# A row-wise nanmax on one core: the wait for the last store moved to GpSimd, into a critical section of its own

One Trainium2 chip, one core of it. The metric is the time of one execution on the device in microseconds (us), the median over several executions. The profile is of one execution; its span runs from the first to the last instruction of the program.

## The reference

```python
def setup_inputs():
    batch, seq, dim = 32, 2048, 2048
    x = np.random.randn(batch, seq, dim).astype(np.float32)
    mask = np.random.rand(batch, seq, dim) < 0.1
    x[mask] = np.nan
    return {"x": x, "axis": -1}

def reference(x, axis):
    return np.nanmax(x, axis=axis).astype(np.float32)
```

537 MB are read and 0.26 MB written, so the kernel is a stream of loads with just enough arithmetic beside it: on the page of the kernel before, the DMA engines are busy for 90% or more in 39 of 40 slices, and the three compute engines for 79 to 93% of the span.

## The kernel before

ScalarE and GpSimd turn NaNs into a very low number by arithmetic on the upper halves of the floats, and VectorE takes the maximum of each row. All loads and stores are issued by SyncE. The kernel does its own synchronization: everything stands in one critical section, in which a small class (`Order`) sets each wait and each semaphore increment. Only the end of the section matters here:

```python
    with tc.tile_critical():
        order = Order(nc)
        # ... loads, ScalarE, GpSimd and VectorE work, all waits explicit (cut) ...
        for (og, bits), e in zip(stores, ready):
            last = order.add(
                "sp",
                nc.sync,
                lambda: nc.sync.dma_start(out=og, in_=bits),
                [e],
                lane="store",
                step=16,
            )
        nc.sync.wait_ge(order.sems[last[0]], last[1])
```

There are five stores on one semaphore. Each adds 16, and the wait is for 80, so for all of them. The framework wraps the section. At its exit the section's *sync engine* (SyncE, unless told otherwise) raises a semaphore (a counter that others wait on), every engine that takes part answers with a drain, and the sync engine collects the answers. I call these the announcement, the drains and the collecting waits. After the last section the program ends with two all-engine barriers, run by GpSimd, with a semaphore clear between them.

## Time and profile before

| | before |
|---|---|
| median of 3 runs | 1253.81 us (1253.79 to 1254.08) |
| span of the profiled run | 1251.8 us |
| last vector instruction ends | 1248.81 us |
| last store: issue begins / has landed | 1248.84 / 1250.50 us |
| landing to end of span ("the tail") | 1.28 us |

The first two rows are the timed runs and the page; the others come from the trace's records of single instructions and of the store's semaphore, which have starts in nanoseconds. The store raises its semaphore in 16 updates; "landed" is the last of them. In the lines shown, DVE is VectorE, ACT ScalarE and POOL GpSimd; SPq, POOLq and PEldq are the sequencers (the instruction queues) of SyncE, GpSimd and TensorE. The prediction below shows the lines of the page and of the last microseconds.

### The profile page before, as it was taken

The page shows a single profiled execution, that of the slowest core. Times are in us where ns is not written, and L with a number is a line of the kernel's source. Part 1 is how long each engine was busy: PE and PEld are TensorE (multiplying, and loading weights), DVE is VectorE, ACT ScalarE, POOL GpSimd, SP SyncE. Part 2 cuts the span into 40 slices and gives each one's busy share as a digit, 9 for nine tenths or more (in the row PEclk, how much of TensorE's full clock was granted, in tenths as well). Part 3 has the DMA queues.
Part 4 walks back from the last instruction along what each step waited for, and adds up shares of the span by engine and source line. Part 5 has one row for each costly group of instructions (what it writes and reads, how often), then busy time and mean ns, then how long its engine had stood idle before and what let it go on. Part 6 is the DMA issues. An engine that isn't in the chain of part 4 may idle for free.

```text
span 1251.8 us, 872 instructions
## 1 busy us (share of the span) xinstructions
DVE 1110.5 (89%) x169; ACT 988.5 (79%) x271; POOL 1166.9 (93%) x239
## 2 busy tenths in 40 slices
DVE  0888989888889988898988888998888899999999
ACT  3777887778787877788777877787777878989997
POOL 2999989998999899998999899989999999999997
DMA  9999999999999999999999999999999999999997
GB/s 415 440 421 429 440 440 440 424 427 440 440 440 427 424 440 440 438 431 421 440 440 438 432 420 440 440 438 434 418 440 440 436 438 421 431 434 426 430 427 289
DMA packets 16279, 537.20 MB, mean 429 GB/s; under 512 B 2448, under 2 KB 2448, under 8 KB 3472
## 3 DMA queue, kind: packets, MB, share of 16 engines
q1 hardware_dynamic: 16272, 537.14, 99.3%
q14 instruction: 7, 0.06, 0.0%
HBM read 536.87 MB, written 0.26 MB: 429 GB/s over the span
## 4 chain that ended last, share of the span: by engine, by line
DVE 37%; DMA 35%; POOL 17%; ACT 10%; issue 1%; SPq 0%; DVEq 0%
DVE acc L194 37%; DMA xt<-in_x_dram 35%; POOL xt L190 17%; ACT kt L186 9%; ACT xt L186 1%; SPq L228 0%; DVE none L194 0%; DVEq L124 0%; SPq L384 0%; SPq L182 0%
## 5 line engine op out<-in xcount | busy, mean ns | idle before, releaser
L190 POOL TENSOR_SCALAR xt<-kt 128x3584 int16<-128x3584 uint16 (+8 forms) x235 | 1166.7, 4965 | 78.7 <-ACT kt L186 60.1
L194 DVE TENSOR_REDUCE acc<-xt 128x3 f32<-128x6144 f32 (+4 forms) x164 | 1108.8, 6807 | 137.1 <-POOL xt L190 127.7
L186 ACT ACTIVATE kt<-xt,scalars 128x3584 uint16<-128x3584 int16 (+9 forms) x248 | 936.0, 3812 | 255.8 <-DMA xt<-in_x_dram 237.9
L186 ACT ACTIVATE xt<-kt 128x3584 int16<-128x3584 uint16 (+4 forms) x21 | 53.5, 2545 | 0.7
L186 ACT ACT_TABLE_LOAD x1 | 1.3, 1283 | 0.9 <-SPq L182 0.9
L196 DVE MEMSET scalars<- 128x1 f32 x1 | 0.1, 59 | 1.0 <-SPq L182 1.0
L194 DVE TENSOR_SCALAR none<-acc 128x414 int32<-128x414 f32 (+1 forms) x2 | 0.9, 428 | 0.1
L194 DVE TENSOR_TENSOR acc<-acc,none 128x414 int32<-128x414 int32 (+1 forms) x2 | 0.8, 422 | 0.1
L370 POOL MEMSET const-float32-0.0<- 128x1 f32 x1 | 0.1, 99 | 0.2 <-issue 0.2
L186 ACT ACTIVATE scalars<-scalars 128x1 f32<-128x1 f32 x1 | 0.2, 202 | 0.0
L370 POOL MEMSET const-bfloat16-1.0<- 128x1 bf16 x1 | 0.1, 102 | 0.0
L370 POOL MEMSET const-uint8-127<- 128x1 uint8 x1 | 0.1, 102 | 0.0
L370 POOL MEMSET const-float32-1.0<- 128x1 f32 x1 | 0.1, 99 | 0.0
## 6 DMA issues: line engine op xcount, KB each, us to landing
xt<-in_x_dram SPq DMA_DIRECT2D x61, 7168.0 KB, 22.5
xt<-in_x_dram SPq DMA_DIRECT2D x12, 1024.0 KB, 27.5
xt<-in_x_dram SPq DMA_DIRECT2D x5, 2048.0 KB, 22.0
xt<-in_x_dram SPq DMA_DIRECT2D x2, 4864.0 KB, 18.9
xt<-in_x_dram SPq DMA_DIRECT2D x2, 3584.0 KB, 22.0
xt<-in_x_dram SPq DMA_DIRECT2D x3, 2304.0 KB, 20.4
xt<-in_x_dram SPq DMA_DIRECT2D x5, 1280.0 KB, 26.3
xt<-in_x_dram SPq DMA_DIRECT2D x1, 4608.0 KB, 18.5
```

The costliest lines, as they stand in the source:

```text
L186: return order.add("act", nc.scalar, lambda: nc.scalar.activation(**kw), deps)
L190: "pool", nc.gpsimd, lambda: nc.gpsimd.tensor_scalar(**kw), deps
L194: return order.add("dve", nc.vector, lambda: do(**kw), deps)
L196: e_top = order.add("dve", nc.vector, lambda: nc.vector.memset(top, EDGE), [])
L370: nc = _bacc.Bacc("TRN2", target_bir_lowering=False, num_devices=1)
```

## The change

The intent: SyncE leaves the first section without waiting for the store, so the section's exit runs while the store is in flight, and one engine alone then waits for the store in a second section.

```diff
                 lane="store",
                 step=16,
             )
-        nc.sync.wait_ge(order.sems[last[0]], last[1])
+
+    with tc.tile_critical(sync_engine=mybir.EngineType.Pool):
+        nc.gpsimd.wait_ge(order.sems[last[0]], last[1])
```

## The prediction

> **What bounds the kernel now.** I read the page first, from the span down to the chain that ended last, then the timeline of the last microseconds, then the sync engine's own waits, and last the instructions of the two lines that make the closing sequence.
>
> ```profile
> span 1251.8 us, 872 instructions
> DVE 1110.5 (89%) x169; ACT 988.5 (79%) x271; POOL 1166.9 (93%) x239
> DMA  9999999999999999999999999999999999999997
> HBM read 536.87 MB, written 0.26 MB: 429 GB/s over the span
> DVE 37%; DMA 35%; POOL 17%; ACT 10%; issue 1%; SPq 0%; DVEq 0%
> ```
>
> The reader is to see that the load stream sets the length. 536.87 MB at 429 GB/s is 1251 us, the whole span, and the row of DMA shares shows the queues over 90% busy in 39 of 40 slices. The three compute engines keep up with it at 79 to 93%. The change touches none of that: it moves one wait that stands after the last store is issued. So the stage to read is the last slice, and in it only what follows the final vector instruction. In the fourth row the sync engine's sequencer (SPq) has 0% of the chain, which already says how little is there.
>
> The timeline of the last microseconds shows where that stage begins:
>
> ```profile
> 1243.70 4.52 DVE L194 TENSOR_REDUCE acc<-xt 128x1 f32<-128x2048 f32 x2
> 1248.25 0.26 DVE L194 TENSOR_SCALAR none<-acc 128x98 int32<-128x98 f32 x1
> 1248.55 0.26 DVE L194 TENSOR_TENSOR acc<-acc,none 128x98 int32<-128x98 int32 x1
> 1248.84 0.33 SPq L348 DMA_DIRECT2D out_dram<-acc  x1
> ```
>
> GpSimd's last piece of work ends at 1245.8 us, ScalarE's at 1245.8, VectorE's at 1248.8. The last store is issued at 1248.84. From there to the end of the span is 1251.8 - 1248.84 = 2.96 us, and all of the change lies inside these 2.96 us, 0.24% of the span. The sync engine's waits split them:
>
> ```profile
> SPq L182 <- DMA out_dram<-acc: 1.3, 1, 1.3
> SPq L384 <- PEq L384: 0.5, 2, 0.4
> ```
>
> The first row is the wait that is moved. It lasts from the end of the issue (1248.84 + 0.33 = 1249.17) to the landing, 1.7 us after the issue began by the DMA issues (1248.84 + 1.66 = 1250.50). What is left, 1251.8 - 1250.5 = 1.3 us, is a closing sequence of semaphores. Its instructions, from the views of lines L182 (first section's exit) and L384 (end of the program) over that window:
>
> ```profile
> L182 SPq COMPARE_BRANCH  x1: 37/37/37, 1250.5 to 1250.5; - x1
> L182 SPq EVENT_SEMAPHORE  x3: 17/17/28, 1250.7 to 1250.9; - x3
> L182 POOLq DRAIN  x1: 41/41/41, 1250.7 to 1250.7; - x1
> L182 SPq NOP  x1: 18/18/18, 1251.0 to 1251.0; - x1
> L384 SPq DRAIN  x3: 7/7/7, 1251.1 to 1251.4; - x3
> L384 POOLq EVENT_SEMAPHORE  x4: 17/17/17, 1251.2 to 1251.7; - x4
> ```
>
> The branch at 1250.5 is the one that waits for the store. The records hold starts to the nanosecond, which narrow windows give to hundredths: branch 1250.51, SyncE's announcement 1250.68, one drain on each of four engines 1250.72 to 1250.77, SyncE's collecting waits 1250.85, 1250.91 and 1250.98, its drains 1251.06 and 1251.13, and GpSimd passing the first all-engine barrier at 1251.16. After that two barriers with a semaphore clear between them take 1251.8 - 1251.16 = 0.6 us; they stay as they are.
>
> [...] 49 KB, 1.7 us to landing. It is the same in both kernels, since the store is still issued by SyncE. [...] the rows have 7 to 41 ns each, yet the steps between them are 40 to 170 ns. I therefore cost steps from start to start, not durations. [...] SyncE's announcement at 1250.68 starts the others' drains at 1250.72, 40 ns. [...] the branch at 1250.51 is followed after 0.165 us, and the one on GpSimd at the start (0.76 to 0.96) after 0.20 us.
>
> **The change part by part.** The comparison of instruction order shows the same instructions on every engine up to the last store; by counts, the program has 8 more on GpSimd, 2 on SyncE and one on each of the others, all behind the last store.
>
> 1. Removed: SyncE's wait for the store before the first section's exit. That exit (announcement, four drains, three collecting waits, a NOP) now starts when the last store is issued, at 1249.17, and needs about what it needs now, 1251.06 - 1250.51 = 0.55 us; it ends near 1249.7, hidden beside the 1.3 us of flight. From the path this takes the 0.55 us from the landing to SyncE's first closing drain. Also GpSimd has been idle since 1245.8, so nothing delays its arrival.
>
> 2. Added before the wait: GpSimd's entry to the second section, a NOP and three waits at about 0.08 us each (two consecutive GpSimd semaphore instructions in the closing barrier start at 1251.16 and 1251.24). All but the last are done by 1250.0, also hidden.
>
> 3. Added after the landing, on the path. GpSimd sees the store at 1250.51 (20 ns after the landing, as SyncE does). Then 0.08 us to its branch, 0.165 to 0.20 us to the instruction after it, its announcement, at 1250.76 to 1250.79. Then two ways run side by side. GpSimd itself: drain +0.08, NOP that waits for its own drain +0.08 to 0.10, final drain +0.08, barrier wait +0.08, so ready at 1251.08 to 1251.13. SyncE: it waits for GpSimd's drain (that drain at 1250.86, 0.04 long, its signal seen 0.02 later at 1250.92), then two drains at +0.07 and +0.06, 1251.05, and the barrier's count full 0.02 later at 1251.07.
>
> 4. Sum. GpSimd passes the first barrier at the later of the two, 1251.08 to 1251.13, against 1251.16 now: the path loses 0.55 + 0.10 us (landing to drain, drain to barrier) and gains 0.57 to 0.62 us. The balance is -0.03 to -0.08 us, call it -0.05 us. What I chose here: I gave the branch on GpSimd the cost of the measured ones, and its drain the 41 ns of the one in the trace.
>
> The load stream and its 1249 us are untouched, so the time is 1253.81 - 0.05 = 1253.76 us; I round to **1253.8**.
>
> **The rivals.** First, a real gain: the whole exit of the first section, 0.55 us, is hidden behind the flight and the second section costs almost nothing. For it speaks that only one engine takes part. Against it: the chain above has a branch, an announcement, a drain and a hand-over to SyncE after the landing, the same kinds of step as before with one hop fewer. It would give 1253.3 us. Second, a loss: GpSimd's sequencer is slower than SyncE's (its drain 41 ns against 7; 0.08 us a step), and the two branches into new blocks could each wait for instructions. The page's instruction queue moves 7 packets in the whole run; [...] my estimate from the 1.7 us store is 1 to 2 us: 1255 to 1256. Against it: [...] GpSimd stands in the wait for over half a microsecond [...]. Third, the change shifts nothing of its own, but another run of a stream at 429 GB/s differs: 0.1% of it is 1.25 us, while the three runs of before lie within 0.29 us. Every version of this stays within 0.3% of 1253.81.
>
> **Range and chances.** The arithmetic allows ±0.6 us; the run-to-run spread of the stream and a possible shift between sessions add about 0.5 to 1 us. I take 1252.8 to 1254.8. 2% would be 25 us, over eight times the 2.96 us in which the change lives. Even removing the whole tail could not make it faster by 2%, and slower by 2% would need a failure the trace has no sign of. Faster 0.005, same 0.985, slower 0.01.
>
> **What would show it right or wrong.** Right: the store's wait stands on GpSimd's sequencer at the new line; the first section's exit (L182) lies before the landing, near 1249.2 to 1249.7; the end of the span follows the landing by 1.2 to 1.3 us; everything up to the last store is alike. Step 1 is wrong if the L182 drains still come after the landing. Step 3 is wrong if the branch to GpSimd's announcement takes over 0.3 us [...] or if the tail falls under 1.0 us. The prediction as a whole fails if the loads' rate or the vector engine's end at 1248.8 shifts by more than a microsecond, which no step of mine gives a cause for.

(Slips of the text: the row with the chain's shares is the fifth of the lines shown, not the fourth. 536.87 MB over 429 GB/s is no test of what bounds the kernel, since the page's rate is the bytes over the span; the row of DMA shares is.)

("49 KB, 1.7 us to landing" is the last store. The sum came to -0.03 to -0.08 us, taken as -0.05, and 1253.81 - 0.05 = 1253.76 us. The second rival, that a branch into a new block could wait for instructions, was a guess, and its 1 to 2 us were my estimate from the 1.7 us of the store; before shows no such wait.)

## The result and the profile after

| | runs | median | lowest to highest |
|---|---|---|---|
| before | 6 | 1253.89 us | 1253.76 to 1254.15 |
| after | 6 | 1253.87 us | 1253.68 to 1254.16 |

The ratio of after to before is 1.000, 95% interval 0.9987 to 1.0013. A ratio is the mean time of one kernel's fast runs over the mean of the other's in the same rounds, so it is not quite the ratio of the medians. The kernel is correct.

The page of the changed kernel, its span, engines and chain:

```profile
span 1252.4 us, 880 instructions
DVE 1110.6 (89%) x169; ACT 988.5 (79%) x271; POOL 1166.3 (93%) x239
DVE 38%; DMA 36%; POOL 16%; ACT 9%; issue 1%; SPq 0%; DVEq 0%
```

The engines are as busy as before. Eight instructions more are recorded, all on GpSimd's sequencer. The span is 0.6 us longer, so the next question is where. The timeline of the changed kernel's last microseconds (start, duration, engine, what):

```profile
1249.17 0.26 DVE L194 TENSOR_TENSOR acc<-acc,none 128x98 int32<-128x98 int32 x1
1249.46 0.33 SPq L348 DMA_DIRECT2D out_dram<-acc  x1
```

The same two lines stood at 1248.55 and 1248.84 before. So the whole 0.62 us was there before the last store was issued, upstream of the first changed instruction. It is not the change: the six runs of the changed kernel span 1251.9 to 1252.4 us, and a second trace of each kernel (below) has the last vector instruction end at 1249.03 (before) and 1249.21 (after). The traced execution of before was a short one (1253.55 us), that of after a long one (1254.14 us).

Behind the store the picture is as intended. From the view of line L182, the first section's exit, in the changed kernel (duration min/median/max in ns, first and last start in us):

```profile
L182 SPq EVENT_SEMAPHORE  x3: 17/17/28, 1249.8 to 1250.1; - x3
L182 POOLq DRAIN  x1: 41/41/41, 1249.9 to 1249.9; - x1
L182 SPq NOP  x1: 18/18/18, 1250.2 to 1250.2; - x1
```

It now lies between the end of the issue (1249.79) and 1250.2, before the landing at 1251.18, and the branch that waited for the store is gone from it. From the views of L354 (the new section) and L386 (end of the program) in the changed kernel:

```profile
L354 POOLq EVENT_SEMAPHORE  x1: 17/17/17, 1251.4 to 1251.4; - x1
L354 POOLq DRAIN  x1: 39/39/39, 1251.5 to 1251.5; - x1
```

```profile
L386 POOLq EVENT_SEMAPHORE  x7: 17/17/742, 1250.3 to 1252.3; - x7
L386 SPq EVENT_SEMAPHORE  x3: 17/17/1327, 1250.2 to 1252.3; - x3
L386 SPq DRAIN  x3: 7/7/7, 1251.6 to 1252.0; - x3
L386 POOLq COMPARE_BRANCH  x1: 33/33/33, 1251.3 to 1251.3; - x1
```

The 742 ns in the first row are GpSimd's wait for the store (1250.47 to 1251.21). The 1327 ns are SyncE waiting for GpSimd's drain. After the landing come GpSimd's branch (1251.25), announcement (1251.40) and drain (1251.50), then SyncE's drains (1251.61 and 1251.67), and GpSimd passes the first barrier at 1251.74. That is 0.566 us after the landing, against 0.662 before. The tail is 1.184 us against 1.279. SyncE's wait in its own list has changed its releaser from the DMA to GpSimd (changed kernel):

```profile
SPq L386 <- POOLq L354: 1.4, 1, 1.4
```

### The profile page after: what moved, and what is told of

It reads as the page before. It is cut to its first block, busy times and chain, and to the rows that moved or that the text cites. A ratio compares the mean times of both kernels' runs of the same rounds, so it can differ in the third digit from the quotient of the medians.

```text
span 1252.4 us, 880 instructions
## 1 busy us (share of the span) xinstructions
DVE 1110.6 (89%) x169; ACT 988.5 (79%) x271; POOL 1166.3 (93%) x239
## 3 DMA queue, kind: packets, MB, share of 16 engines
HBM read 536.87 MB, written 0.26 MB: 429 GB/s over the span
## 4 chain that ended last, share of the span: by engine, by line
DVE 38%; DMA 36%; POOL 16%; ACT 9%; issue 1%; SPq 0%; DVEq 0%
DVE acc L194 38%; DMA xt<-in_x_dram 36%; POOL xt L190 16%; ACT kt L186 8%; ACT xt L186 1%; SPq L228 0%; DVE none L194 0%; SPq L386 0%; SPq L182 0%; DVEq L124 0%
```

## The experiments

**Theories.** Mine: the change trades one sequence of semaphore steps after the landing for a slightly shorter one; what counts is how many steps stand between the landing and the first barrier, and what stands before the landing is hidden as long as it fits into the flight. Rivals: the section of its own is what helps; the waiting engine is what matters; a section of one engine is nearly free, or waits for instructions in each new block; and the 0.6 us longer span belongs to the change.

The main measure is read from each trace: the time from the landing of the last store to GpSimd's passing of the first barrier, and to the end of the span. Single executions scatter by some tenths of a microsecond upstream of the store, so the time itself cannot resolve 0.1 us.

| kernel | landing to first barrier | landing to end | flight of the store | last vector instruction ends |
|---|---|---|---|---|
| before | 0.662 | 1.279 | 1.66 | 1248.81 |
| before_again | 0.662 | 1.279 | 1.70 | 1249.03 |
| after | 0.566 | 1.184 | 1.72 | 1249.43 |
| after_again | 0.574 | 1.193 | 1.75 | 1249.21 |
| own_sp | 0.532 | 1.149 | 1.86 | 1249.09 |
| own_pe | 0.747 | 1.374 | 1.72 | 1249.19 |
| same_pool | 0.425 | 1.042 | 1.90 | 1249.04 |
| one_ahead | 0.674 | 1.293 | 1.72 | 1249.06 |
| two_ahead | 1.493 | 2.111 | 1.71 | 1249.12 |
| eight_after | 7.017 | 8.081 | 1.72 | 1249.08 |

(All in us; flight is from the start of the issue.) All kernels gave correct results, and the granted clock was 1.000 in every run. before_again, own_pe, one_ahead and two_ahead were executed once each (1253.81, 1254.09, 1253.89 and 1254.75 us, beside one run of before at 1254.01 us). The state of a single run is unknown, so only their traces are used.

A limit of this measure: the flight is not constant, and it scatters by as much as the tails differ. In all ten traces the packets of the store end 1.14 to 1.15 us after the start of the issue and the first of its 16 updates comes at 1.36 to 1.37; only the later updates scatter. From the start of the issue to the end of the span it is 2.94 and 2.98 us in before, 2.91 and 2.94 in after, 2.94 in same_pool and 3.01 in own_sp. The flight was longer in every changed kernel than in the two traces of before; whether that is chance is not shown. What the traces show is a shorter way behind the landing, not a shorter program.

**before_again and after_again: both kernels unchanged.**

> The kernel before once more, for its tail. Theory: the first barrier passes 0.66 us after the landing and the span ends 1.28 us after it, both within 0.02 us of the first trace, so that the 0.09 us between the two kernels' tails is no accident of one trace. Rival: they vary by 0.1 us or more from trace to trace.

> The changed kernel once more, for the spread of its tail and of its time. Theory (the change only trades two short semaphore sequences after the landing): the time from the landing of the last store to the end of the span repeats at 1.18 us within 0.03 us, as in the first trace after (1251.18 to 1252.36), while the moment of the landing wanders by up to 0.6 us with the load stream; ratio 1.000 within 0.0005. Rival (the 0.6 us longer span of the first trace after belongs to the change): the span is again about 1252.4 us and the last vector instruction again ends 0.6 us later than the 1248.81 us of before.

From the view of L182 in the second trace of before, the waiting branch and SyncE's last step:

```profile
L182 SPq COMPARE_BRANCH  x1: 38/38/38, 1250.8 to 1250.8; - x1
L182 SPq NOP  x1: 18/18/18, 1251.2 to 1251.2; - x1
```

Branch to NOP takes the same 0.47 us as in the first trace, and the tail of before repeated at 1.279 us. That of after came to 1.193 against 1.184 us. So the difference of 0.09 us is no accident of one trace. The last vector instruction of the second after ended 0.22 us earlier than in the first, with nothing changed, and its span was 1252.2 us. That is still 0.4 us above the first trace of before, so this trace alone does not settle the rival that gives the longer span to the change. The timed runs do: the five of after_again span 1252.0 to 1252.2 us, the nine of before beside them 1252.1 to 1252.3 us. The rival falls. In time, after_again had a median of 1253.86 us (5 runs) beside 1254.04 us of before (9 runs), ratio 0.9999, interval 0.9986 to 1.0011.

**same_pool: GpSimd waits, but inside the first section.**

```diff
-        nc.sync.wait_ge(order.sems[last[0]], last[1])
+        nc.gpsimd.wait_ge(order.sems[last[0]], last[1])
```

(against before)

> Half of the change: GpSimd waits, but inside the first section, with no section of its own. Theory (what counts is the number of hand-overs after the landing): after the landing stand the branch, GpSimd's drain, SyncE's NOP and two drains, so the first closing barrier passes about 0.42 us after the landing (0.66 before, 0.57 after) and the tail is about 1.03 us against 1.28 and 1.18. In time this is 0.15 us below the changed kernel, under the spread. Rival (the section of its own is what hides the first exit): the tail is 1.28 us as before, since SyncE again leaves the section only when the store has landed.

From the view of L182 in this kernel:

```profile
L182 SPq EVENT_SEMAPHORE  x3: 17/17/28, 1249.5 to 1249.7; - x3
L182 POOLq COMPARE_BRANCH  x1: 33/33/33, 1251.0 to 1251.0; - x1
L182 POOLq DRAIN  x1: 41/41/41, 1251.2 to 1251.2; - x1
L182 SPq NOP  x1: 18/18/18, 1251.2 to 1251.2; - x1
```

SyncE has announced and collected the other drains by 1249.7, long before the landing at 1250.97. Only GpSimd's answer is missing, and when it comes one NOP and two drains of SyncE's follow. The barrier passes at 0.425 us, as expected from the theory (0.42). The rival expected 1.28 us for the tail and got 1.042. So here the first exit is hidden by the waiting engine not being the one that announces. A section of its own isn't needed for that; it costs about 0.14 us (0.566 and 0.574 against 0.425). In time: median 1253.79 us (5 runs) beside 1254.04 us, ratio 0.9997, interval 0.9984 to 1.0011. This is the shortest tail that I found, 0.24 us below before, but the time does not show it beyond doubt: its five runs (1253.54 to 1253.84 us) all lie below the nine of before beside them (1253.85 to 1254.08), yet before has also been measured at 1253.76, and in the trace the long flight (1.90 us) took the gain back.

**own_sp: a section of its own, with SyncE waiting.**

```diff
-    with tc.tile_critical(sync_engine=mybir.EngineType.Pool):
-        nc.gpsimd.wait_ge(order.sems[last[0]], last[1])
+    with tc.tile_critical(sync_engine=mybir.EngineType.SP):
+        nc.sync.wait_ge(order.sems[last[0]], last[1])
```

(against after)

> The other half: a section of its own, but with SyncE alone as the waiting engine. Theory: branch 0.17, announcement to drain 0.07, NOP 0.06, two drains 0.13 and the barrier 0.03 after 0.09 us for wait and branch: the first barrier passes about 0.55 us after the landing, tail about 1.16 us, like the changed kernel within 0.05 us. Rival (the engine is what matters, GpSimd's sequencer being slower at 0.08 us a step): tail at or under 1.0 us.

From the view of L354 in this kernel:

```profile
L354 SPq EVENT_SEMAPHORE  x1: 17/17/17, 1251.2 to 1251.2; - x1
L354 SPq DRAIN  x1: 7/7/7, 1251.3 to 1251.3; - x1
```

The landing was at 1250.98, and announcement and drain follow at 0.225 and 0.314 us after it. The barrier passes at 0.532 us, which is the theory's 0.55 and close to the 0.566 and 0.574 of GpSimd. The rival's tail of 1.0 us or less did not come (1.149). Median 1253.93 us (5 runs) beside 1254.04 us, ratio 0.9999, interval 0.9987 to 1.0012.

**own_pe: a section of its own, with TensorE's sequencer waiting.** The same edit as in own_sp, with `EngineType.PE` and `nc.tensor.wait_ge`.

> The section of its own with TensorE's sequencer as the waiting engine, which does nothing else in this kernel. Theory (number of hand-overs): as many as in the changed kernel, the first barrier passes 0.52 to 0.65 us after the landing. Rival (the engine matters: TensorE's semaphore instructions are recorded with 51 ns against GpSimd's 17): over 0.75 us.

From the view of L386 in this kernel:

```profile
L386 PEldq COMPARE_BRANCH  x1: 173/173/173, 1251.0 to 1251.0; - x1
```

This was a miss. The barrier passes at 0.747 us, out of the range that I gave to the theory (0.52 to 0.65) and just under the rival's 0.75. TensorE's branch takes 173 ns where GpSimd's and SyncE's take 33 to 41; from branch to announcement it needs 0.23 us (0.15 on GpSimd) and from announcement to drain 0.19 (0.095). So the number of steps is not all: the same steps on TensorE are slow enough to make the tail longer than before (1.374 us). Between SyncE and GpSimd the engine matters little (0.03 to 0.04 us); with TensorE it does. Why its steps are slower is not shown.

**eight_after: eight more sections behind the wait.**

```diff
+    for _ in range(8):
+        with tc.tile_critical(sync_engine=mybir.EngineType.Pool):
+            nc.gpsimd.wait_ge(order.sems[last[0]], last[1])
```

(appended to after)

> Eight more sections of GpSimd alone behind the wait, each waiting for the same store, so that the cost of one section can be read in the time. Theory (a section of one engine costs its own chain of semaphore instructions and one branch, about 0.7 us, worked out from the steps of the first trace after): plus 5 to 6.5 us, about 1259.5 us, ratio 1.0045, with 0.6 to 0.8 us between one announcement and the next. Rival A (a section of one engine is nearly free): under 1 us in all. Rival B (each new block waits for instructions): over 1.5 us a section, plus 12 us or more.

From the view of L357 (the added sections) and that of L389 (end of the program) in this kernel:

```profile
L357 POOLq NOP  x16: 13/13/13, 1251.4 to 1257.7; - x16
L357 POOLq EVENT_SEMAPHORE  x8: 17/17/17, 1251.9 to 1257.5; - x8
```

```profile
L389 POOLq COMPARE_BRANCH  x9: 32/33/41, 1250.9 to 1257.4; - x9
L389 POOLq DRAIN  x3: 34/64/182, 1257.8 to 1258.5; - x3
L389 POOLq EVENT_SEMAPHORE_RANGE_CLEAR  x1: 69/69/69, 1258.1 to 1258.1; - x1
```

Eight announcements lie from 1251.88 to 1257.51, seven steps of (1257.51 - 1251.88) / 7 = 0.80 us, all alike. That is the top of what I expected (0.6 to 0.8). The time rose to a median of 1260.79 us (4 runs) beside 1254.04 us, ratio 1.0054, interval 1.0040 to 1.0068. The 6.9 us over after_again (1260.79 - 1253.86) are a little more than I expected (5 to 6.5): the sections give 8 x 0.80 = 6.4 us. Of the rest, 0.3 us is a stretch of 0.40 us between the start of the semaphore clear and the drain behind it (1258.10 to 1258.50), which takes 0.10 to 0.11 us in the other traces, and 0.15 us is that drain itself (182 ns against 34). The DMA view has no packet of the instruction queue between 1248 us and the end of the span, so the trace does not put it down to a load of instructions. The cause stays open. Each section's branch cost 0.15 us and a whole section 0.80, so the 1.5 us of rival B did not come (that figure lies within the prediction's estimate of 1 to 2 us; no trace shows such a wait), and a section is not nearly free (rival A).

**one_ahead and two_ahead: one or two more sections before the wait.**

```diff
+    for _ in range(1):   # 2 in two_ahead
+        with tc.tile_critical(sync_engine=mybir.EngineType.Pool):
+            nc.gpsimd.wait_ge(order.sems["load0"], 16)
     with tc.tile_critical(sync_engine=mybir.EngineType.Pool):
         nc.gpsimd.wait_ge(order.sems[last[0]], last[1])
```

> One more section of GpSimd alone, put before the wait for the store; it waits for a load that landed a millisecond earlier. Theory (what stands before the wait is hidden as long as it fits into the flight of the store): GpSimd now reaches the wait 0.68 us after the issue of the store has ended (trace of the changed kernel), a section takes 0.80 us (eight_after), so it would reach it at 1.48 us, and the store lands 1.33 to 1.6 us after the end of the issue: 0 to 0.15 us come to the surface, and the first closing barrier passes 0.55 to 0.72 us after the landing (0.57 without). Rival (a section is paid for wherever it stands): 1.37 us after the landing.

> Two such sections before the wait. Theory: GpSimd reaches the wait at 0.68 + 2 x 0.80 = 2.28 us after the end of the issue, the store lands at 1.33 to 1.6 us, so 0.7 to 0.95 us come to the surface and the first barrier passes 1.25 to 1.5 us after the landing. Rival (paid for wherever it stands): 2.17 us. If both runs agree with the theory, the exit of the first section was truly hidden in the change.

From the view of L389 in one_ahead, then in two_ahead (compare the longest wait in the changed kernel, 742 ns):

```profile
L389 POOLq EVENT_SEMAPHORE  x10: 17/30/43, 1249.9 to 1252.0; - x10
L389 POOLq COMPARE_BRANCH  x2: 33/33/33, 1250.2 to 1251.0; - x2
```

```profile
L389 POOLq EVENT_SEMAPHORE  x13: 17/43/43, 1250.0 to 1252.9; - x13
L389 POOLq COMPARE_BRANCH  x3: 33/33/33, 1250.2 to 1251.9; - x3
```

No wait of GpSimd's is longer than 43 ns now: the store has already landed when it is asked for. In one_ahead GpSimd reaches the wait 1.49 us after the end of the issue (expected 1.48) and the store had landed at 1.39, so 0.10 us come to the surface: the barrier passes at 0.674 us, against a mean of 0.570 in the two traces of after. In two_ahead it is 2.30 us (expected 2.28) against 1.38, so 0.92 us, and the barrier passes at 1.493. The rival expected 1.37 and 2.17. One section of 0.80 us costs 0.10 us there and the second the full 0.82: what stands before the wait is hidden up to the end of the flight and paid for in full after it. The changed kernel had about 0.7 us of that room left over (0.80 - 0.10).

What was not tried: taking the wait away, which would end the program with a store in flight (my estimate from the traces: the exit's NOP at 1250.18 in after, plus the 0.79 us from that NOP to the end in before, is 1250.97 us, and the store landed at 1251.18); and a wait outside of any section, which the framework refused to build (it reported a deadlock).

## Why the prediction was right

The time was predicted as 1253.8 us and measured as 1253.87; within 2% was given 0.985. The number alone proves little: 1253.8 is also what no effect at all gives, and the first rival's 1253.3 lies within the range of 1252.8 to 1254.8. What can be right or wrong is the mechanism. Its parts, one by one:

1. *Load stream untouched.* Right. Busy times and shares are the same, and what moved upstream of the store (0.62 us) is the difference between a short and a long execution; the spans of the timed runs overlap.
2. *The first exit is hidden (step 1 of the prediction).* Right, shown by the L182 lines and by one_ahead and two_ahead. Its length was oversized: it ran from 0.05 to 0.41 us after the end of the issue, not 0.55, since no waiting branch stands in it any more. Nothing depends on that, as it is hidden. The entry to the second section (step 2) was hidden as well: GpSimd stood in its last wait 0.71 us before the landing.
3. *New steps after the landing (step 3).* The mechanism was right, and GpSimd's own arrival, not SyncE's, was the later of the two ways, as argued: the barrier passed 84 ns after GpSimd's final drain and 74 ns after SyncE's, and where SyncE's is the last to come (before, own_sp, same_pool), 32 to 33 ns are enough. Three terms were sized too high: landing to branch took 0.074 us (0.09 was used), branch to announcement 0.152 (0.165 to 0.20), and GpSimd's NOP to its final drain 0.042 (0.08). Two were too low: announcement to drain took 0.095 us (0.08), and drain to NOP 0.119 (0.08 to 0.10). So the barrier passed 0.566 and 0.574 us after the landing instead of 0.58 to 0.63.
4. *Sum (step 4).* -0.03 to -0.08 us was predicted, -0.09 to -0.10 came (0.662 to 0.574 and 0.566). The sign holds and the size is a little over the range. In time it can't be seen. The flight was taken to be the same in both kernels; in the traces it was 1.66 and 1.70 us before and 1.72 and 1.75 after, which takes back more than half of the gain in these traces (that the change causes it is not shown). In the first trace of before, 0.84 of the 1.66 us lie before the first packet, 0.31 are packets, and 0.51 come after the last one.
5. *Rivals of the prediction.* The full gain of 0.55 us did not come, because the second section puts its own chain in the place of the first one's; same_pool shows that 0.24 of it was to be had, behind the landing, by a smaller edit. The second rival's loss did not come: from GpSimd's branch to its announcement passed 0.152 us (over 0.3 was the prediction's mark against step 3), and the last packet of the instruction queue in the two traces of after is at 1247.7 and 1247.8 us, before the last store. The spread between runs (0.29 us over the first three runs of before) is three times the effect.

The prediction's mark of a tail of "1.2 to 1.3 us" was missed by a hair (1.184 and 1.193).

## What to carry to other kernels

Where a change moves a wait at the end of a program, lay out the chain from the landing of the last transfer to the end, start to start, and count what stands behind it: here everything before the landing was free, as long as it fitted into the flight (of two sections of 0.80 us put before the wait, the first cost 0.10 us and the second 0.82). Here it paid to let an engine wait that the section's exit asks last (GpSimd; 0.425 us to the first barrier in same_pool), and not the one that announces the exit (SyncE; 0.662 in before); a section of its own added steps (0.566 and 0.574 in the two traces of after). And before any of it compare what follows the last issue (3 us here) with the span (1252 us): a change there is worth tenths of a microsecond, which only the trace can measure, and the flight of the store scatters by as much.

## What the traces show of single steps

- A wait can stand outside the record or inside it. The branch that waits for the store has 37 and 38 ns on SyncE in the two traces of before and 33 ns on GpSimd in same_pool, after more than a microsecond of waiting. Of the semaphore instructions in the changed kernel, one is recorded with 742 ns on GpSimd and one with 1327 ns on SyncE, the wait inside.
- A compare-and-branch at the end of a section is recorded with 32 to 41 ns on SyncE and GpSimd and 173 ns on TensorE, and from its start to that of the next instruction it is 0.15 to 0.17 us on the first two and 0.23 us on TensorE.
- Consecutive semaphore waits that were already met start 0.05 to 0.06 us apart on SyncE (own_sp), 0.07 to 0.09 on GpSimd (after) and 0.11 on TensorE (own_pe). A whole critical section of GpSimd alone is 0.80 us (eight_after), and 0.81 us ahead of the wait (one_ahead).
- Of the 16 semaphore updates of the last store (49 KB), the first comes 1.36 to 1.37 us after the start of the issue and the last 1.66 to 1.90 us (ten traces).
